# Low-rank stage ahead of the recurrence, gemms in thirds beside it, and an even spread of output projections over the last recurrence

## The chip, the cores and the metric

The kernel runs on one core of a Trainium2 chip. The metric is the device time of one execution in microseconds (us); the time before is the median of three runs. Profiles are of one execution each. Engines: PE is TensorE's matmuls (PEld its weight loads), DVE VectorE, ACT ScalarE, POOL GpSimd, SP SyncE, whose queue issues most DMAs. The granted clock is the share of full TensorE clock that the throttle allowed.

## The reference, cut to what matters

One inference step of a two-layer trunk for a prompt of 1024 tokens and 8 sample streams of 16 tokens, width 1024, all float32. Layer 0 is an RWKV-7 time mixing and an FFN, layer 1 a banded attention and an FFN; every sub-layer is modulated by `silu(c) @ w_ada`. The change lies in the time mixing of layer 0:

```python
r = xr @ w_r;  k = xk @ w_k;  v = xv @ w_v
w_log = -softplus(-(w0 + tanh(xw @ w1) @ w2)) - 0.5      # low rank
a_gate = sigmoid(a0 + (xa @ a1) @ a2)                    # low rank
g = sigmoid(xg @ g1) @ g2                                # low rank
# for each token: the 64x64 state of each of 16 heads
s = s * w_t + (s @ a_t) b_t + v_t k_t ;  y = s @ r_t
y = groupnorm(y) * ln_w + ln_b + bonus
x = x + gate * ((y * g) @ w_o)
```

## The kernel before, in words

The 1152 tokens (1024 of the prompt, 128 of the samples) are cut into three blocks of 384. Precise products are made of float32r halves: a weight tile is loaded raw (512 KB), ACT copies it to a high half (`whi`), DVE subtracts for the low half (`wlo`), and each product is three matmuls (`mm3`, line 257). A gemm of one output tile (`gemm`, line 263) is 8 k steps, 24 matmuls into one bank `acc`.

**Projection of a block** (`proj`, line 495) is a generator whose steps are its yields: the low-rank stage `proj_lora` (line 545; seven yields: three first-stage products, two of gates, two of outputs), then `proj_k` (670), then the inverses of the block's three windows in alternation with `proj_r` (523), then `proj_v` (638); each of the three big ones is 8 gemms, with one yield after each. Results go to DRAM (`spill`, `save`) and are loaded again by the recurrence.

**The recurrence** goes window by window (128 tokens; 9 windows, each in two halves of the heads, so 18 units). A unit is prepared (`win_prep`, line 785: masked products in two banks `G`), run (`win_run`, `win_state`: for each of two chunks of 64 tokens a product X, an eviction, U with the inverse TT, an eviction, D, and the new state, in two banks `st`), summed in bank `Y`, and normed (`win_post`, line 1018: mean and variance by matmuls into two more `st` banks; the result goes to DRAM as `yg`). The two units of a pair are woven, so that one waits while the other works. The inverse of a window (`inverses`, line 773) is a chain of its own: products, a DMA to DRAM, a solve of 15 steps on DVE, DMAs, and four merges in `st` banks.

**The modulation steps** (`ada_steps`, line 195): 8 units of four loads of 512 KB, each with 4 small matmuls, and an end with a copy on ACT. 8 steps are taken in `proj_v` of block 2, 24 are left. They share the raw buffers of `rawtile` (line 227) with the weights; behind block 2 there are two such buffers (line 1170).

**The order** is written in `layer0a` (line 1156). Block 0 is projected alone. For blocks 1 and 2, `alternate` (line 1061) takes 5 steps of the recurrence of the block before, then 4 of the projection. Behind block 2 the last six units run, 5 steps of them to 2 of `early` (line 1173), which holds the 24 modulation steps and then `outproj` (line 1130) of blocks 0 and 1; `outproj` of block 2 comes last. The program is built with `schedule_with_timeline_sim=True`: the instructions are put in order for each engine from this text, and what an engine executes need not be in the text's order.

An output projection loads `yg` (8 tiles `mr`, split into 16 tiles `mx`), runs 8 gemms with the weights `rw_o`, adds the residual, and ends with a square sum whose result is stored as `rr`.

Of the kernel before, what the change touches and what calls it, by code (L numbers as in the profile page):

```python
# [16 lines left out]
NB = 3  # L17
TB = 384
KF = 8
KAPPA = float(np.exp(-0.5))  # L20


# [119 lines left out]
class Trunk:  # L142
# [44 lines left out]
        return self.ps.tile([128, 512], dt, tag=tag, name=self.nm(tag), bufs=bufs)  # L187


    def step(self, n=1):  # L190

        for _ in range(n):
            next(self.ada, None)

    def ada_steps(self, units, tag="aux", bufs=1, tile=None):

        nc = self.nc
        for u in units:
            ps = self.bank(tag, bufs)
            for i in range(4):  # L200
                w = (tile or self.rawtile)()
                nc.sync.dma_start(w[:, :1024], self.a["wada"][u, i])
                c = slice(i // 2 * 256, i // 2 * 256 + 256)
                for q in range(4):
                    mm(nc, ps[32 * q:32 * q + 32, c], self.scT[:, i % 2 * 4 + q, :], w[:, q * 256:q * 256 + 256], i % 2 == 0, i % 2 == 1)
                if i < 3:
                    yield
            sb = (tile or self.rawtile)()[:, :512]
            nc.scalar.activation(sb, ps, AF.Copy)
            for j in range(4):  # L210
                mm(nc, ps[:, j * 16:(j + 1) * 16], sb[:, j * 128:(j + 1) * 128], self.C("qs"), True, True)
            pv = ps[:, 0:64].rearrange("p (j n) -> p j n", n=16)[:, :, 0:9]
            bo = PAR["bada"] + u * 4
            bv = self.par[:, bo:bo + 4].rearrange("p (j o) -> p j o", o=1).broadcast_to([128, 4, 9])
            nc.vector.tensor_tensor(self.mod[:, u * 4:u * 4 + 4, :], pv, bv, ALU.add)
            yield
# [46 lines left out]
    def gemm(self, out, W, hi, lo, m=128):  # L263

        whi, wlo = W
        for k in range(8):
            s = slice(k * m, (k + 1) * m)
            self.mm3(out, whi[:, s], wlo[:, s], hi[k], lo[k], k == 0, k == 7)


    def sq_open(self):
        return Ctx()
# [250 lines left out]
    def proj_r(self, b, hi, lo):  # L523

        nc = self.nc
        for f in range(8):
            W = self.wunit(self.pp, self.a["rw_r"][f])
            pz = self.bank("acc", 2)
            self.gemm(pz[:, :TB], W, hi, lo)
            kp = self.ev("ag", 2)  # L530
            self.load(kp, "kp", b, f)
            ex = self.ev("rr", 2)
            self.load(ex, "cs", b, f)
            nc.scalar.activation(ex, ex, AF.Exp, scale=-KAPPA)
            nc.vector.scalar_tensor_tensor(kp, pz[:, :TB], self.P("rk", f), kp, ALU.mult, ALU.mult)
            nc.vector.tensor_tensor(ex, ex, pz[:, :TB], ALU.mult)
            self.spill("r", b, f, ex)
            aux = self.bank("aux", 1)
            mm(nc, aux[:, :TB], self.C("bo"), kp, True, True)
            bn = self.ev("e0", 3)  # L540
            nc.scalar.activation(bn, aux[:, :TB], AF.Copy)
            self.save("bn", b, f, bn)
            yield
# [94 lines left out]
    def proj_v(self, b, hi, lo):  # L638

        nc = self.nc  # L640
        for f in range(8):
            W = self.wunit(self.pp, self.a["rw_v"][f])
            pz = self.bank("acc", 2)
            self.gemm(pz[:, :TB], W, hi, lo)
            if b in (2,):
                self.step(1)
            vv = self.ev("vv", 2)
            self.load(vv, "bn", b, f)
            v = self.ev("e0", 3)
            nc.scalar.activation(v, pz[:, :TB], AF.Copy)  # L650
            nc.vector.tensor_tensor(vv, vv, pz[:, :TB], ALU.mult)
            nc.scalar.activation(vv, vv, AF.Identity, bias=self.P("lnb", f))
            self.spill("v", b, f, vv)
            pt = self.bank("aux", 1)
            for w in range(3):
                nc.tensor.transpose(pt[:, w * 128:(w + 1) * 128], v[:, w * 128:(w + 1) * 128], self.C("ident"))
            vt = self.ev("e0", 3)
            nc.scalar.activation(vt, pt[:, :TB], AF.Copy)
            for e in range(2):
                nc.sync.dma_start(self.sv[b][:, :, e, f, :].rearrange("w p d -> p w d"),  # L660
                                  vt.rearrange("p (w e d) -> p e w d", w=3, e=2)[:, e])
            yield
# [7 lines left out]
    def proj_k(self, b, hi, lo):  # L670

        nc = self.nc
        self.eend = self.eends[b]
        for f in range(8):
            W = self.wunit(self.pp, self.a["rw_k"][f])
            pz = self.bank("acc", 2)
            self.gemm(pz[:, :TB], W, hi, lo)
            iv = self.ev("rr", 2)
            self.load(iv, "cs", b, f)
            ag = self.ev("ag", 2)  # L680
            self.load(ag, "a", b, f)
            ext = self.pp.tile([128, 408], F32, tag="ext", name=self.nm("ext"), bufs=1)
            for s, sx, n, i in self.spans(b):
                ev = ext[:, sx].rearrange("p (g t) -> p g t", t=n + 1)
                nc.gpsimd.memset(ev[:, :, 0:1], 1.0)
                nc.scalar.activation(ev[:, :, 1:], iv[:, s].rearrange("p (g t) -> p g t", t=n), AF.Exp, scale=-KAPPA)
                nc.gpsimd.tensor_copy(self.eend[:, f, i:i + ev.shape[1]], ev[:, :, n])
            nc.scalar.activation(iv, iv, AF.Exp, scale=KAPPA)
            sq = self.ev("sq", self.nsq)
            kk = self.ev("kk")  # L690
            nc.scalar.activation(sq, pz[:, :TB], AF.Square, scale=self.P("kk", f))
            aux = self.bank("aux", 1)
            mm(nc, aux[:, :TB], self.C("bo"), sq, True, True)
            kp = self.ev("kp")
            nc.scalar.activation(kp, ag, AF.Identity, bias=self.oka[:, f:f + 1], scale=self.P("ka", f))
            inv = self.ev("inv", self.nsq)
            nc.vector.tensor_scalar(inv, aux[:, :TB], 1e-24, None, ALU.max)
            nc.scalar.activation(inv, inv, AF.Ln)
            nc.scalar.activation(inv, inv, AF.Exp, scale=-0.5)
            nc.vector.tensor_tensor(kp, kp, pz[:, :TB], ALU.mult)  # L700
            self.save("kp", b, f, kp)
            nc.vector.scalar_tensor_tensor(kk, pz[:, :TB], self.P("kk", f), inv, ALU.mult, ALU.mult)
            nc.vector.tensor_tensor(ag, ag, kk, ALU.mult)
            for s, sx, n, i in self.spans(b):
                seg = kk[:, s].rearrange("p (g t) -> p g t", t=n)
                nc.vector.scalar_tensor_tensor(seg, seg, -1.0, ext[:, sx].rearrange("p (g t) -> p g t", t=n + 1)[:, :, 0:n],
                                               ALU.mult, ALU.mult)
            self.spill("kk", b, f, kk)
            nc.vector.tensor_tensor(ag, ag, iv, ALU.mult)
            self.spill("b", b, f, ag)  # L710
            nc.vector.tensor_tensor(iv, iv, kp, ALU.mult)
            self.spill("k", b, f, iv)
            yield
# [304 lines left out]
    def win_post(self, w, hf, R):  # L1018
# [11 lines left out]
        mm(nc, cen, self.C("cen"), y, True, True)  # L1030
        nc.scalar.activation(y, cen, AF.Square)
        yield
        var = self.bank("st", 2)
        mm(nc, var, self.C("bo"), y, True, True)
        nc.scalar.activation(y, var, AF.Ln, bias=self.eps[:, 1:2], scale=1.0 / 64)
        nc.scalar.activation(y, y, AF.Exp, scale=-0.5)
# [93 lines left out]
    def outproj(self, b):  # L1130
# [12 lines left out]
        for f in range(8):  # L1143
            W = self.wunit(pp, self.a["rw_o"][f])
            pz = self.bank("acc", 2)
            self.gemm(pz[:, :TB], W, hi, lo)
            x = self.ev("rr")
            nc.sync.dma_start(x, self.a["x"][b][:, f, :])
            o = self.ev("e0")
            self.residual(256 if b == 2 else TB, f, 16, o, x, pz[:, :TB])  # L1150
            nc.sync.dma_start(self.x1[:, f, cols], o)
            self.sq_add(st, o)
            yield
        nc.sync.dma_start(self.rr[:, cols], self.sq_done(st))

    def layer0a(self, ctx):
# [4 lines left out]
        with ExitStack() as c2:  # L1161
# [2 lines left out]
                pass  # L1164
            for b in range(1, NB):
                w = self.windows([(w, hf) for w in range(3 * b - 3, 3 * b) for hf in range(2)])
                for _ in self.alternate(w, self.proj(b), 5, 4):
                    pass
        self.tail_open(ct)
        self.nraw, self.nhi, self.nlo = (2, 2, 2)  # L1170
        self.nmix, self.nmr = 16, 2

        def early():
            for _ in range(32):
                if next(self.ada, StopIteration) is StopIteration:
                    break
                yield
            for b in range(2):
                yield from self.outproj(b)
        for _ in self.alternate(self.windows([divmod(int(x), 2) for x in '12 13 16 14 15 17'.split()]), early(), 5, 2):  # L1180
            pass
        cw.close()
        for _ in self.outproj(2):
# [743 lines left out]
```

## Time and profile before

| what | value |
|---|---|
| median of 3 runs | 3878.44 us (3875.95 to 3879.47) |
| the profiled execution | 3879.81 us; its span 3878.0 us |
| mean granted clock | 0.926 |
| block 0 alone (first weights of block 1's low-rank stage are loaded at 277 us) | 0 to 277 us |
| blocks 1 and 2 with the recurrence of the block before | 277 to 985 us |
| the last recurrence and the output projections | 985 to 1342 us |
| everything else (two FFNs, attention) | 1342 to 3878 us |
| DMA moved | 552.31 MB, mean 142 GB/s |

The profile gives busy time of the engines, the granted clock, and for each idle time of an engine what ended it. A busy PE is not PE at its peak: at half clock the same matmuls keep it busy for twice as long, so busy share and clock are read together.

### The profile page before, as it was taken

The numbers are of one execution on the slowest core, as the hardware profiler recorded it, in microseconds if no ns is written. First come the engines' busy times: TensorE is split into PE (matmuls) and PEld (weight loads), VectorE is DVE, ScalarE is ACT, GpSimd is POOL, SyncE is SP. The second block draws the span as 40 slices with busy tenths as digits, with TensorE's granted clock in tenths as the row PEclk, the third lists the DMA queues.
The fourth block names the chain that finished last, engine by engine and source line by source line (L and its number), as shares of the span: only waits on it lengthen the run. The fifth ranks groups of instructions, "written<-read, shape, count | busy, mean of one in ns | idle before, by whom it ended". The sixth has DMA issues, their size and how long they took to land.

```text
span 3878.0 us, 72281 instructions
## 1 busy us (share of the span) xinstructions
PE 3545.9 (91%) x28614; PEld 3130.7 (81%) x28614; DVE 2292.3 (59%) x4388; ACT 1570.7 (41%) x2966; POOL 570.8 (15%) x473
## 2 busy tenths in 40 slices
PE   6789889988889799999999999889889799999999
PEld 4677777867657689999887879677677799999898
DVE  4667566765435765555456842666675764555567
ACT  5555555544213533333311353465654533333310
POOL 0000000000000255444000100000000264453000
PEclk8896899798679989999999999899999899999999
DMA  5775676676646522222755113444554322222521
GB/s 205 229 237 159 182 220 170 176 219 185 185 142 194 175 71 71 75 77 77 270 192 187 68 59 100 140 141 141 150 191 162 127 79 74 74 75 92 170 84 71
DMA packets 429443, 552.31 MB, mean 142 GB/s; under 512 B 128432, under 2 KB 297520, under 8 KB 424624
## 3 DMA queue, kind: packets, MB, share of 16 engines
q1 hardware_dynamic: 374960, 528.80, 42.8%
q10 hardware_dynamic: 54144, 18.89, 2.1%
q8 instruction: 225, 3.69, 0.4%
q14 instruction: 114, 0.93, 0.1%
HBM read 413.42 MB, written 134.12 MB: 141 GB/s over the span
## 4 chain that ended last, share of the span: by engine, by line
PE 67%; DMA 11%; DVE 7%; ACT 4%; issue 2%; SPq 1%; POOL 0%; ACTq 0%; DVEq 0%; POOLq 0%
PE S L139 31%; PE PT L139 15%; PE acc L139 10%; PE st L139 3%; PE O L139 2%; PE G L139 2%; DVE h L255 1%; PE PT L1753 1%; PE Y L139 1%; PE aux L139 1%; DMA TT<-Z 1%; DMA raw<-in_wada 1%; DMA mr<-yg 1%; DMA yg<-y 1%; DMA rr<-sf_cs 1%
## 5 line engine op out<-in xcount | busy, mean ns | idle before, releaser
L139 PE MATMUL S<-h,w 128*128 128x320 f32 (+1 forms) x4944 | 696.9, 300 | 17.9 <-DVE h L255 8.3
L139 PEld LDWEIGHTS S<-h,w 128*128 128x128 f32 x4944 | 675.5, 192 | 26.0 <-DVE h L255 13.3
L139 PE MATMUL S<-h,wh 128*128 128x320 f32 (+1 forms) x2844 | 529.7, 338 | 12.7 <-DVE h L1123 6.8
L139 PE MATMUL acc<-mx,whi 128*128 128x384 f32 x1728 | 497.4, 366 | 30.3 <-ACT mx L254 12.7
L139 PEld LDWEIGHTS S<-h,wh 128*128 128x128 f32 x2844 | 455.7, 189 | 69.2 <-issue 13.3
L254 ACT ACTIVATE w<-rq 128x512 fp32r<-128x512 f32 x308 | 192.1, 629 | 502.4 <-PE S L139 199.3
L255 DVE TENSOR_TENSOR w<-rq,w 128x512 fp32r<-128x512 f32 x308 | 270.6, 882 | 199.1 <-ACT w L254 198.4
L139 PEld LDWEIGHTS acc<-mx,whi 128*128 128x128 f32 x1728 | 332.6, 201 | 60.5 <-ACT mx L254 15.6
L139 PE MATMUL PT<-h,w 128*128 128x320 f32 (+1 forms) x2448 | 355.0, 300 | 15.1 <-ACT w L254 6.9
L139 PEld LDWEIGHTS PT<-h,w 128*128 128x128 f32 x2448 | 337.4, 192 | 18.9 <-ACT w L254 7.1
L139 PE MATMUL acc<-mx,wlo 128*128 128x384 f32 x864 | 311.3, 361 | 6.6 <-DVE wlo L255 6.5
L139 PE MATMUL PT<-h,wh 128*128 128x320 f32 (+1 forms) x1428 | 287.6, 345 | 9.6 <-DVE wh L255 3.9
L1312 POOL TENSOR_TENSOR t<-t,t 128x576 f32<-128x576 f32 (+1 forms) x132 | 216.1, 1637 | 414.2 <-ACT t L1319 291.7
L139 PEld LDWEIGHTS PT<-h,wh 128*128 128x128 f32 x1428 | 234.2, 191 | 39.0 <-issue 6.9
L255 DVE TENSOR_TENSOR wlo<-raw,whi 128x1024 fp32r<-128x1024 f32 x114 | 139.9, 1230 | 96.4 <-ACT whi L254 89.3
L139 PEld LDWEIGHTS acc<-mx,wlo 128*128 128x128 f32 x864 | 172.5, 200 | 14.0 <-DVE wlo L255 9.6
L254 ACT ACTIVATE whi<-raw 128x1024 fp32r<-128x1024 f32 x114 | 119.5, 1054 | 143.0 <-PE acc L139 96.4
L255 DVE TENSOR_TENSOR h<-h,h 128x1024 fp32r<-128x1024 f32 (+4 forms) x112 | 122.9, 1112 | 84.7 <-ACT h L254 69.7
L254 ACT ACTIVATE h<-h 128x1024 fp32r<-128x1024 f32 (+4 forms) x112 | 103.2, 935 | 164.1 <-DMA h<-sd 105.3
L254 ACT ACTIVATE wh<-rq 128x512 fp32r<-128x512 f32 x124 | 74.8, 626 | 230.6 <-PE S L139 146.3
L1312 DVE TENSOR_TENSOR t<-S,t 128x576 f32<-128x576 f32 (+1 forms) x116 | 86.4, 745 | 128.5 <-PE S L139 128.5
L1379 DVE TENSOR_TENSOR h<-h,S 128x640 f32<-128x640 f32 (+1 forms) x150 | 112.1, 752 | 79.4 <-PE S L139 79.2
(423 smaller groups left out, 5712.9 us busy)
## 6 DMA issues: line engine op xcount, KB each, us to landing
h<-in_wada SPq DMA_DIRECT2D x64, 512.0 KB, 6.3
rq<-in_wg SPq DMA_DIRECT2D x88, 256.0 KB, 2.6
rq<-in_wu SPq DMA_DIRECT2D x88, 256.0 KB, 2.6
rq<-in_wd SPq DMA_DIRECT2D x88, 256.0 KB, 3.0
raw<-in_wada SPq DMA_DIRECT2D x32, 512.0 KB, 4.6
kc<-in_ck SPq DMA_DIRECT2D x16, 1024.0 KB, 5.1
vc<-in_cv SPq DMA_DIRECT2D x16, 1024.0 KB, 7.2
sd<-t SPq DMA_DIRECT2D x88, 160.0 KB, 1.9
```

The costliest lines, as they stand in the source:

```text
L139: return nc.tensor.matmul(out, lhsT, rhs, start=start, stop=stop)
L254: self.nc.scalar.activation(hi, x, AF.Copy)
L255: self.nc.vector.tensor_tensor(lo, x, hi, ALU.subtract)
L1312: eng.tensor_tensor(out, x, y, ALU.add)
L1379: nc.vector.tensor_tensor(y, y, d, ALU.add)
L1753: nc.tensor.transpose(pt[:, j * 128:(j + 1) * 128], P[:, j * 128:(j + 1) * 128], self.C("ident"))
```

## The change

Five edits, one of them used at several places:

- `gemm_steps` replaces `gemm` in `proj_r`, `proj_v`, `proj_k` and `outproj`. It is the same 24 matmuls, with a yield after the third and the sixth k step; a gemm is now three steps.
- For blocks 1 and 2, seven steps of the projection (the low-rank stage) are taken ahead of the alternation, and the alternation is 2 steps of the recurrence to 3 of the projection.
- The variance in `win_post` takes a bank of `G` in place of one of `st`.
- Behind block 2, `early` alternates `outproj(0)` and the modulation steps one to one, then `outproj(1)`; the last recurrence takes 1 step to 2 of `early`.
- From there on the load of a modulation step is written one step ahead (`fetch_ahead`).

```diff
+LOW = 7
...
+        def load(u, i):
+            w = (tile or self.rawtile)()
+            nc.sync.dma_start(w[:, :1024], self.a["wada"][u, i])
+            return w
+        todo = [(u, i) for u in units for i in range(4)]
+        ahead = None
...
-                w = (tile or self.rawtile)()
-                nc.sync.dma_start(w[:, :1024], self.a["wada"][u, i])
+                w = ahead or load(*todo.pop(0))
+                ahead = load(*todo.pop(0)) if todo and self.fetch_ahead else None
...
+    def gemm_steps(self, out, W, hi, lo):
+
+        whi, wlo = W
+        for k in range(8):
+            s = slice(k * 128, (k + 1) * 128)
+            self.mm3(out, whi[:, s], wlo[:, s], hi[k], lo[k], k == 0, k == 7)
+            if k in (2, 5):
+                yield
...
-            self.gemm(pz[:, :TB], W, hi, lo)
+            yield from self.gemm_steps(pz[:, :TB], W, hi, lo)
...
-        var = self.bank("st", 2)
+        var = self.bank("G", 2)
...
-                for _ in self.alternate(w, self.proj(b), 5, 4):
+                p = self.proj(b)
+                for _ in range(LOW):
+                    next(p)
+                for _ in self.alternate(w, p, 2, 3):
                     pass
         self.tail_open(ct)
+        self.fetch_ahead = True
...
         def early():
-            for _ in range(32):
-                if next(self.ada, StopIteration) is StopIteration:
-                    break
-                yield
-            for b in range(2):
-                yield from self.outproj(b)
-        for _ in self.alternate(self.windows([divmod(int(x), 2) for x in '12 13 16 14 15 17'.split()]), early(), 5, 2):
+            yield from self.alternate(self.outproj(0), self.ada, 1, 1)
+            yield from self.outproj(1)
+        for _ in self.alternate(self.windows([divmod(int(x), 2) for x in '12 13 16 14 15 17'.split()]), early(), 1, 2):
             pass
```

More of the change, by code (lines that the diff above doesn't have):

```diff
@@ L187, in bank @@
         return self.ps.tile([128, 512], dt, tag=tag, name=self.nm(tag), bufs=bufs)
+    fetch_ahead = False
     def step(self, n=1):
@@ L643, in proj_v @@
             pz = self.bank("acc", 2)
-            self.gemm(pz[:, :TB], W, hi, lo)
+            yield from self.gemm_steps(pz[:, :TB], W, hi, lo)
             if b in (2,):
@@ L676, in proj_k @@
             pz = self.bank("acc", 2)
-            self.gemm(pz[:, :TB], W, hi, lo)
+            yield from self.gemm_steps(pz[:, :TB], W, hi, lo)
             iv = self.ev("rr", 2)
@@ L1145, in outproj @@
             pz = self.bank("acc", 2)
-            self.gemm(pz[:, :TB], W, hi, lo)
+            yield from self.gemm_steps(pz[:, :TB], W, hi, lo)
             x = self.ev("rr")
```

## The prediction

> **What bounds the kernel now.** I read the page first: span, engine shares, and the slices with the granted clock.
>
> ```profile
> span 3878.0 us, 72281 instructions
> PE 3545.9 (91%) x28614; PEld 3130.7 (81%) x28614; DVE 2292.3 (59%) x4388; ACT 1570.7 (41%) x2966; POOL 570.8 (15%) x473
> PE   6789889988889799999999999889889799999999
> PEclk8896899798679989999999999899999899999999
> ```
>
> TensorE bounds the kernel: 91% busy, the next engine 59%. A slice is 97 us, so the change touches only slices 1 to 14, up to 1345 us; what follows (the first FFN, the attention, the second FFN) is left as it is and I forecast nothing for it. In the early slices both rows are lower than later. The stages there, in one table of the stretches (columns: stretch, length, then busy us and count of PE, PEld, DVE, ACT, sometimes POOL, then granted clock, DMA share, GB/s):
>
> ```profile
> 84.00:115.00 31.00, 21.80 (x65) 14.53 (x63) 23.79 (x36) 21.87 (x40) 0.00 (x0) 0.70 0.66 218
> 332.00:400.00 68.00, 61.38 (x564) 49.95 (x563) 47.89 (x111) 28.37 (x54) 0.00 (x0) 0.53 0.49 142
> 684.00:735.00 51.00, 48.40 (x473) 38.37 (x472) 40.94 (x83) 28.17 (x53) 0.00 (x0) 0.56 0.59 173
> 400.00:621.00 221.00, 199.77 (x2367) 167.47 (x2366) 146.46 (x325) 122.28 (x237) 2.90 (x19) 0.92 0.68 200
> 735.00:985.00 250.00, 221.82 (x2705) 182.74 (x2702) 149.44 (x332) 119.12 (x236) 6.15 (x30) 0.92 0.71 201
> 985.00:1176.00 191.00, 162.55 (x1784) 118.55 (x1784) 72.28 (x191) 43.18 (x88) 0.00 (x0) 0.68 0.56 156
> 1236.00:1345.00 109.00, 84.47 (x409) 75.50 (x408) 76.75 (x135) 54.33 (x101) 19.69 (x16) 0.91 0.58 185
> ```
>
> The first three rows are the second half of the low-rank stage (gates and outputs, `proj_lora`) of blocks 0, 1 and 2; the next two are the gemms of blocks 1 and 2 beside the recurrence of the block before; then comes the last recurrence with the modulation steps, and last what is left of the output projections. Three things stand out. The same low-rank half takes 31 us alone, 68 and 51 us beside the recurrence's preparation, and there the clock is 0.53 and 0.56. The last recurrence runs for 191 us at 0.68 with no gemm beside it. After it, 109 us hold little but output projections.
>
> The text's order is a priority and not the order of execution: the zeroing matmul of the first recurrence unit, which stands in the text behind the whole of block 0, runs at 2.40 us.
>
> ```profile
> 2.40 0.79 PE L139 MATMUL Y<-zr 128*128 128x512 f32 x1 [2.40 <-ACT zr L735]
> ```
>
> So an edit that only moves steps in the text moves the time only where readiness and buffers let it. I price each part from what stands in its way.
>
> **A. The low-rank stage ahead (LOW = 7).** Seven steps are exactly `proj_lora`: three first-stage products, two gates, two outputs. What lies between them in blocks 1 and 2 is the preparation of the next recurrence units (tile G) and merges of the last inverse (tile st). First three rows of PE alone for the tile acc, then two for G, then two of all engines for st:
>
> ```profile
> 84.00:115.00 31.00, 21.80 (x65) 0.70 0.66 218
> 332.00:400.00 68.00, 27.17 (x68) 0.53 0.49 142
> 684.00:735.00 51.00, 25.10 (x66) 0.56 0.59 173
> 332.00:400.00 68.00, 27.08 (x128) 0.53 0.49 142
> 684.00:735.00 51.00, 18.98 (x96) 0.56 0.59 173
> 332.00:400.00 68.00, 9.66 (x368) 8.62 (x368) 2.80 (x8) 2.75 (x9) 0.53 0.49 142
> 684.00:735.00 51.00, 6.01 (x311) 5.33 (x312) 1.14 (x4) 2.38 (x8) 0.56 0.59 173
> ```
>
> The acc matmuls are the same 64 or so each time. If the stage runs alone it takes block 0's 31 us: (68 - 31) + (51 - 31) = 57 us less. The displaced work, 27.1 + 19.0 + 9.7 + 6.0 = 62 us of PE at a clock of about 0.545, then stands beside the gemms at 0.92: 62 x 0.545 / 0.92 = 37 us. Net 57 - 37 = 20 us. The other end is 0: the preparation is ready, and may slip into the idle places of the low-rank stage as before. I take 14, nearer to block 0's row, since that is the same stage with nothing beside it. Its DMAs (the loads of the low-rank weights, the saves of its results) now go ahead of the preparation's loads on SP's queue; I cost that at nothing, because the first state step runs only here, behind the merges:
>
> ```profile
> 415.43 1.15 PE L139 MATMUL st<-UV,XL 128*64 128x64 f32 x32
> 747.29 1.15 PE L139 MATMUL st<-UV,XL 128*64 128x64 f32 x32
> ```
>
> That is 15 and 12 us after the low-rank stage ends. If this cover goes, a late start is paid at most with those stretches' idle time, below.
>
> The Trainium skill, page "TensorE: Matmul & The Clock Gate", section "Why this matters for your kernels", says that a TensorE kept busy some 4 us without a break gets the full clock. This trace differs: 48.4 of 51 us busy, and 0.56 granted. By the rule moving the preparation would win no clock, and this part would come to 62 - 57 = 5 us lost.
>
> **B. Gemms in thirds, 2:3 instead of 5:4, and the variance in bank G.** No matmul is added. Each gemm (24 matmuls) gets two more places for a recurrence step, and the inverses alternate with thirds of `proj_r`, in block 0 too, where I cost it at nothing (the gemms of `proj_v` follow without a wait on it). What can be won is the idle time of the two gemm stretches, 221 - 199.8 + 250 - 221.8 = 49 us. Of it these waits are what a finer weave or a freed st bank would shorten (in 400 to 985: total, times, longest):
>
> ```profile
> PE st L139 <- ACT y L1028: 5.1, 2, 4.8
> PE st L139 <- ACT UV L943: 4.2, 4, 2.2
> PE st L139 <- ACT y L1031: 3.7, 3, 1.4
> PE st L139 <- ACT xs L934: 2.8, 3, 1.4
> PE G L139 <- DVE XL L819: 5.8, 1, 5.8
> ```
>
> The first four sum to 16 us. The last is the price of the bank: the variance matmul now waits in PE's queue until a mask multiply on DVE has freed a G bank, once 5.8 us, and queued behind it is every later matmul. I take half of the 16, 8 us; the ends are 16 won and the loss of rival 3.
>
> **C. The end of the stage.** Now the 24 remaining modulation steps come first, then output projections 0 and 1, then 2 after the last window. Rows of the tile raw, and of SP's queue (start, us):
>
> ```profile
> L202 SPq DMA_DIRECT2D raw<-in_wada x24: 327/338/859, 1016.6 to 1165.8; - x24
> L209 ACT ACTIVATE raw<-aux x6: 592/597/606, 1039.3 to 1171.7; 128x512 f32<-128x512 f32 x6
> 1171.74 6.47 SPq L247 DMA_DIRECT2D raw<-in_rw_o  x3
> 1246.17 0.34 SPq L1154 DMA_DIRECT2D rr<-rms  x1
> 1267.49 0.33 SPq L247 DMA_DIRECT2D raw<-in_rw_o  x1
> 1275.89 0.33 SPq L247 DMA_DIRECT2D raw<-in_rw_o  x1
> 1287.03 0.33 SPq L1154 DMA_DIRECT2D rr<-rms  x1
> 1341.78 0.32 SPq L1154 DMA_DIRECT2D rr<-rms  x1
> 1244.77 0.37 ACTq L1043 DMA_DIRECT2D yg<-y  x1
> ```
>
> Everything goes through two raw buffers: 24 loads and 6 copies in 1171.7 - 1016.6 = 155 us, 5.17 us a buffer; the weights of a projection running alone, with one more load between the two quoted, (1275.89 - 1267.49) / 2 = 4.2 us. A projection ends where its rr is stored: 0 at 1246, 1 at 1287 (41 us later), 2 at 1342 (55 us later). The windows end at 1245.
>
> Alternating 1:1 puts projection 0 among the modulation steps. The buffers still carry 30 + 8 = 38 tiles: 30 x 5.17 + 8 x 4.2 = 189 us, to 1206; with an estimated 6 us for the last tile's split and gemm (one and a half of the 4.2) projection 0 ends at 1212, projection 1 at 1253 beside the last windows, projection 2 at 1308: 34 us earlier. PE has room: projection 0's 8 gemms are 41 us at most by projection 1's row, and 985 to 1176 has 28 us idle and runs at 0.68. The modulation load a step ahead is no new buffer, so it can only pull the pace towards 4.2; behind it in SP's queue stand the recurrence's loads. What the queues pay now (SP, PE, PE):
>
> ```profile
> SPq L202 <- PE aux L139: 42.6, 13, 10.2
> PE aux L139 <- DMA raw<-in_wada: 17.8, 10, 4.2
> PE G L139 <- DMA BK<-sp_k: 6.6, 3, 5.0
> ```
>
> Its bounds: at 4.2 for all 38, projection 0 ends at 1182, and then the windows decide (rival 2); the loss is rival 4.
>
> **Sum.** 14 + 8 + 34 = 56 us. The profiled execution took 3879.8 us (1.8 outside the span): 3823.8. It lies 1.4 above the median, so 3822.
>
> **Rivals.**
> 1. Nothing moves: the order follows readiness, the buffers carry the same 38 tiles, and projection 0 stays behind. For it: the matmul at 2.40 us. Against: 109 us of projections behind the windows. 3878.
> 2. More is won. With gemms among its steps the last recurrence runs at 0.92 instead of 0.68: 162.6 x (1 - 0.68 / 0.92) = 42 us, the windows end at 1203, projection 1 at 1182 + 41 = 1223, projection 2 at 1278, 64 us earlier. With A at 20 and B at 16: 100 us, 3778. Against: the chain's evictions and DMAs don't follow the clock.
> 3. The thirds cost clock. A gemm that is broken twice and then waits for a recurrence step leaves PE idle in the middle. The stretches hold 199.8 + 221.8 = 422 us of PE at 0.92. At 0.80, half way to the 0.68 of the recurrence without gemms, that is 422 x (0.92 / 0.80 - 1) = 63 us; with A and C, 63 - 48 = 15 slower: 3893. It decides below a clock of 0.83. For it stands the skill's same page, section "HAM oscillation — how this bites in real kernels": run all K tiles through before PE waits. Against: two acc banks hold a second gemm ready.
> 4. Slower through the raw buffers. A matmul whose load is late holds PE's queue and with it the recurrence: 17.8 / 10 = 1.78 us a time, now in 10 of 24 steps. If all 38 tiles pay it, the pace is 5.17 + 1.78 = 6.95: 264 us, projection 0 ends at 1287, projection 2 at 1383, 41 us late; with A and B, 41 - 22 = 19 slower: 3897. C turns to a loss above (1341.8 - 55 - 41 - 6 - 1016.6) / 38 = 5.87 us a tile, the whole above 6.45.
>
> **How the numbers follow.** Forecast 0.50, rival 1 0.12, rival 2 0.21, rival 3 0.06, rival 4 0.11. A difference of 0.2% (8 us) is about what a measurement of this kernel can tell from none. Faster 0.71, same 0.12, slower 0.17. The range is 3770 (a little past rival 2) to 3890 (past rival 1, and the milder part of rivals 3 and 4).
>
> **What would show it.** A: gates and outputs of blocks 1 and 2 in about 31 us, no G among them. B: a clock of 0.92 or more and less than 49 us idle in the gemm stretches. C: weights of the output projections loaded between 1016 and 1206 on the scale of now, the gap from the last yg to the last rr well under today's 97 us. I am wrong if the pace of the raw buffers passes 5.87 us, if the windows end later after the end of block 2's gemms than now, or if the gemm stretches lose clock.

## The result, and the profile after

The changed kernel takes 3939.84 us (median of 4 runs, 3935.16 to 3945.3) against 3877.19 us for the kernel before on the same chip: a ratio of 1.0172, 95% interval 1.0152 to 1.0192, so 63 us slower where 56 us faster was forecast, and outside the forecast range of 3770 to 3890 us. First the page of the changed kernel: span, engines, and the slices with the granted clock.

```profile
span 3933.3 us, 72242 instructions
PE 3573.6 (91%) x28614; PEld 3148.4 (80%) x28614; DVE 2296.6 (58%) x4388; ACT 1579.2 (40%) x2972; POOL 576.4 (15%) x473
PE   5889989898799689999999999888889889999999
PEclk8887988798779679999999999999999999999999
```

The same 28,614 matmuls, the same busy share and much the same clock, in a span 55.3 us longer. A slice is now 98 us. The 6 in the clock's row that stood in the 11th slice, at the last recurrence without gemms, stands in the 14th, behind 1278 us. The stages, cut where they fall in this kernel (columns as in the prediction):

```profile
332.00:387.00 55.00, 50.06 (x532) 39.41 (x532) 44.53 (x102) 27.74 (x54) 0.00 (x0) 0.61 0.60 168
649.00:726.00 77.00, 65.43 (x763) 49.54 (x761) 47.26 (x107) 45.51 (x77) 0.00 (x0) 0.65 0.51 157
735.00:985.00 250.00, 218.08 (x2494) 183.19 (x2492) 136.13 (x291) 112.57 (x225) 4.98 (x28) 0.91 0.65 186
1190.00:1330.00 140.00, 117.58 (x1144) 89.59 (x1143) 68.13 (x152) 36.21 (x63) 0.00 (x0) 0.82 0.41 129
1330.00:1395.00 65.00, 42.68 (x179) 38.17 (x180) 48.56 (x90) 31.84 (x64) 19.54 (x16) 0.74 0.43 141
```

The gates and outputs of blocks 1 and 2 now take 55 and 77 us (before 68 and 51), not 31. In 735 to 985 us TensorE is about as busy as before at about the same clock, but it executes 2494 matmuls where it executed 2705. The gemms' are as many (548 in tile acc, before 552); fewer are those of the recurrence and the inverses (1240 in st for 1319, 294 in G for 336). In 400 to 621 us the gemms have more than before (537 for 504) and st has fewer (872 for 1076). So the projections come early and the recurrence late. The last weights of block 2's `proj_v` are loaded at 937.13 us (before 976.19), the last recurrence store `yg` and the ends `rr` of the three output projections stand here (start in us):

```profile
937.13 0.58 SPq L257 DMA_DIRECT2D raw<-in_rw_v  x1
1325.97 0.37 ACTq L1062 DMA_DIRECT2D yg<-y  x1
1205.76 0.33 SPq L1173 DMA_DIRECT2D rr<-rms  x1
1268.70 0.33 SPq L1173 DMA_DIRECT2D rr<-rms  x1
1393.44 0.32 SPq L1173 DMA_DIRECT2D rr<-rms  x1
```

Projections 0 and 1 end 40 and 18 us earlier than before (1246, 1287). The recurrence ends 81 us later (1326 against 1245), and projection 2, which needs it, 52 us later: nearly the whole loss of the span. The question for the experiments is what holds the recurrence. I call the last store of block 0's, of block 1's and of the last recurrence the three marks: before 653, 977, 1245; changed 715, 1088, 1326.

### The profile page after: what moved, and what is told of

Read it like the earlier page. It is cut to its first block, busy times and chain, and to the rows that moved or that the text cites. A ratio compares the mean times of both kernels' runs of the same rounds, so it can differ in the third digit from the quotient of the medians.

```text
span 3933.3 us, 72242 instructions
## 1 busy us (share of the span) xinstructions
PE 3573.6 (91%) x28614; PEld 3148.4 (80%) x28614; DVE 2296.6 (58%) x4388; ACT 1579.2 (40%) x2972; POOL 576.4 (15%) x473
## 4 chain that ended last, share of the span: by engine, by line
PE 68%; DMA 10%; DVE 7%; ACT 5%; issue 2%; SPq 1%; POOL 1%; ACTq 0%; DVEq 0%; POOLq 0%
PE S L140 31%; PE PT L140 15%; PE acc L140 11%; PE st L140 3%; PE G L140 2%; PE O L140 2%; DVE h L265 1%; PE PT L1772 1%; PE Y L140 1%; PE aux L140 1%; DMA TT<-Z 1%; DMA Z<-T 1%; DMA yg<-y 1%; ACT pts L1773 0%; DMA L<-ld 0%
## 5 line engine op out<-in xcount | busy, mean ns | idle before, releaser
L140 PE MATMUL acc<-mx,whi 128*128 128x384 f32 x1728 | 515.1, 378 | 66.4 <-ACT mx L264 28.7
L140 PEld LDWEIGHTS acc<-mx,whi 128*128 128x128 f32 x1728 | 345.6, 209 | 102.9 <-ACT mx L264 34.4
```

The source lines that it names most:

```text
L140: return nc.tensor.matmul(out, lhsT, rhs, start=start, stop=stop)
```

## The experiments

Each was timed in turn with the kernel before on the same chip; the ratio is to that, with its 95% interval. Line numbers differ by up to 19 between kernels, since the edits add lines.

**1. Inverses thinner in the text?** In the changed kernel an inverse alternates with thirds of `proj_r`, one to one. If its merges were crowded, one step to three thirds would mend it.

```diff
-        yield from self.alternate(self.inverses(b), self.proj_r(b, *r))
+        yield from self.alternate(self.inverses(b), self.proj_r(b, *r), 1, 3)
```

> The changed kernel with one edit: the inverses alternate 1 step to 3 thirds of proj_r, as many as they had to a whole gemm before. Theory (ring): the merges of the inverses, now written three times as close, stand ahead of recurrence steps in the two-bank ring st and hold both banks while they wait for their solve and its DMAs. It expects the last yg of block 0's recurrence near 655 us instead of 714, that of block 1's near 985 instead of 1088, and a time of 3800 to 3860. Rival (priority): the recurrence is late because the low-rank stage and the gemm thirds stand ahead of it; it expects no move, 3920 to 3950. Rival (tail): the raw buffers in the last recurrence cost it; 3920 to 3950.

3933.55 us, 1.0124 (1.0092 to 1.0156); marks 774, 1097, 1324. The inverses did move (that of block 2's last window began its solve at 1047 us instead of 1074), but the recurrence did not come earlier with them: block 0's last store came 59 us later, the other two marks moved by 9 us at most. That theory fell.

**2. The merges of the inverses out of `st`.** The four merges take banks of `G`, and the variance goes back to `st`.

```diff
-        m = self.bank("st", 2)
+        m = self.bank("G", 2)
...
-        var = self.bank("G", 2)
+        var = self.bank("st", 2)
```

> The changed kernel with the four banks of a merge taken from G instead of st, and the variance back in st. The order of the steps in the text is that of the changed kernel. Theory (ring): X, U and D no longer stand behind a merge, only the preparations do, a pair ahead of need: block 1's last yg near 1000 us, 3820 to 3880. Rivals (priority, tail): 3920 to 3960.

3937.18 us, 1.0131 (1.0100 to 1.0162); marks 718, 1067, 1341. No better. What I had not thought of is that this puts another chain into `G` (see 11 to 13).

**3 and 4. The tail alone, and the blocks alone.** The change cut in two: the kernel before with `early`, the 1:2, the thirds in `outproj` and the load ahead; and the changed kernel with the old tail.

> The kernel before with the change's tail alone: outproj in thirds, outproj(0) one to one with the modulation steps, 1 to 2, loads a step ahead; variance in st, blocks 0 to 2 as before. Theory (ring) and the rival (priority): the tail is sound where the recurrence comes to it in time, 3835 to 3865, last yg of all near 1240 us. Rival (tail): 3900 to 3940.

> The change without its tail: behind block 2 all is as before (whole gemms in outproj, 24 modulation steps first, 5 to 2). Theory (ring) and the rival (priority): block 1's last yg stays near 1088 us, the old tail follows it, 3930 to 3990. Rival (tail): the gain of the two blocks shows, 3840 to 3870.

The tail alone: 3884.81 us, 1.0008 (0.9990 to 1.0027), no difference; marks 646, 978, 1276, projections at 1190, 1241, 1342. The blocks alone: 3920.31 us, 1.0083 (1.0051 to 1.0116); marks 724, 1090, 1320. Neither time lies in a range that was expected. Both halves fail to give what was forecast, so there is more than one cause.

**5 to 8. Which of the blocks' edits.** The changed kernel with only the variance put back in `st`; then the kernel before with one edit each: the variance in `G`; the seven low-rank steps ahead (5:4 and whole gemms kept); thirds and 2:3.

```diff
# 5: changed kernel                     # 6: kernel before, the same line reversed
-        var = self.bank("G", 2)
+        var = self.bank("st", 2)
# 7: kernel before
+                p = self.proj(b)
+                for _ in range(7):
+                    next(p)
-                for _ in self.alternate(w, self.proj(b), 5, 4):
+                for _ in self.alternate(w, p, 5, 4):
# 8: kernel before, gemm_steps in proj_k, proj_r, proj_v
-                for _ in self.alternate(w, self.proj(b), 5, 4):
+                for _ in self.alternate(w, self.proj(b), 2, 3):
```

> The changed kernel with one thing undone: the variance of the output norm goes back from a G bank to the st banks. Three theories of why blocks 1 and 2 now end their recurrence late. Variance bank: the centred copy holds one of the two st banks while the variance waits for a G bank behind the chunk preparations and the inverse products, so one st bank is left for the state products and the merges; then this kernel gets most of it back, about 3880 to 3895, with block 1's last store of the recurrence near 1000 (before 977, changed 1088). Priority by the low-rank steps ahead: stays at 3925 to 3940. Thinner spread by thirds and 2:3: stays at 3925 to 3940.

> The kernel before with one thing of the change: the variance of the output norm takes a G bank in place of an st bank. Variance bank: slower by 25 to 40 us, block 0's last store of the recurrence at 700 or later (before 653). Priority by the low-rank steps ahead, and thinner spread by thirds: no difference within 10 us.

> The kernel before with one thing of the change: the seven low-rank steps of the next block stand ahead of the alternation of recurrence and projections; whole gemms and 5:4 as before, the variance in st. Priority by the low-rank steps ahead: slower by 20 to 40 us, with the recurrence of block 0 ending past 680. Variance bank and thinner spread: the same, or faster by up to the 14 us that the prediction gave this part.

> The kernel before with one thing of the change: the projections' gemms in thirds and 2:3 in place of whole gemms and 5:4; no low-rank steps ahead, the variance in st, the tail as before. Thinner spread: slower by 20 to 40 us, with the inverses' or the recurrence's ends of block 0 later by tens of us. Variance bank and priority by the low-rank steps: the same within 10 us.

| kernel | median us | ratio (interval) | marks |
|---|---|---|---|
| 5 changed, variance in `st` | 3887.12 | 1.0015 (1.0002 to 1.0028) | 696, 1046, 1281 |
| 6 before, variance in `G` | 3910.11 | 1.0074 (1.0059 to 1.0089) | 640, 1012, 1302 |
| 7 before, low-rank ahead | 3853.88 | 0.9920 (0.9897 to 0.9942) | 651, 990, 1265 |
| 8 before, thirds and 2:3 | 3876.13 | 0.9983 (0.9965 to 1.0001) | 667, 1006, 1250 |

The variance's bank is the blocks' cost: put back it recovers 1.57 of the 1.72%, alone it costs 0.74%. The low-rank steps ahead are a gain, the thirds make no difference to speak of; both rival theories fell. But the variance theory missed its own mark: block 0's recurrence in kernel 6 ends at 640 us, earlier than before, where I expected 700 or later. Number 5's block 1 ends at 1046 us, where I expected about 1000. The bank costs, and not by the way I thought.

**9 and 10. The two good edits together, and low-rank ahead with the tail.** Kernel 9 is the kernel before with low-rank ahead, thirds and 2:3; kernel 10 is number 7 with the change's tail.

> The kernel before with the low-rank steps ahead, thirds and 2:3 in the blocks; the variance in st, the tail as before. If the parts add (low-rank alone -25.7, thirds alone -3.4): 3845 to 3860, block 1's last store of the recurrence by 1006. If low-rank steps ahead and thirds hinder each other: 3870 to 3890 and that store at about 1046, as in the changed kernel with the variance put back.

> The kernel before with two things of the change: the seven low-rank steps ahead and the tail; whole gemms and 5:4 in the blocks, the variance in st. If the parts add (low-rank alone -25.7 and tail alone +5.2 against the kernel before): 3855 to 3865, the last windows ending about 31 us later than with the low-rank steps alone (1265), at 1290 or more. If the tail gives its gain back only where the windows begin early: the time falls below 3850.

Kernel 9: 3858.36 us, 0.9938 (0.9910 to 0.9966); marks 691, 1030, 1224, projection 2 at 1327. The time adds up within the intervals, though block 1's last store comes at 1030 us and not by 1006; and with kernel 7 it beats both kernels of this case. A late mark in blocks 0 and 1 is thus no loss in itself: 691 and 1030 are later than before (653, 977). Kernel 10: 3876.67 us, 0.9979 (0.9959 to 0.9999); marks 656, 999, 1282: with low-rank ahead the tail costs about 0.6%, more than it did alone. Neither expectation had that.

**11. What the variance's bank costs by.** If the centred copy holding an `st` bank were to blame, taking both banks of the norm from `G` would free `st` and mend it.

```diff
-        cen = self.bank("st", 2)
+        cen = self.bank("G", 2)
...
-        var = self.bank("st", 2)
+        var = self.bank("G", 2)
```

> The kernel before with both banks of the output norm, the centred copy's and the variance's, taken from G, so that the norm holds no st bank. If the variance in G costs because the centred copy holds an st bank while the variance waits: the 30 us are gone, 3875 to 3892, block 1's last store of the recurrence by 990. If a wait for a G bank costs by itself (the norm's matmuls in front of others on the engine, or the chunk preparations kept from their banks): 3905 or more.

3991.65 us, 1.0292 (1.0261 to 1.0322); marks 702, 1083, 1389. Four times the cost: the held `st` bank is not the cause, the use of `G` is. (The norm's two `st` banks are not two others, as "into two more `st` banks" above may read, but turns of the one pair that the state chain and the merges use.) In the kernel before, two things share the two `G` banks: the preparation of the units, and the products that open a window's inverse (`Aab<-G`, copied out by ACT). The latter run ahead of the recurrence. Here are ACT's copies for the middle window of block 1 and the norms of the last units of block 0 (start, us), first in the kernel before:

```profile
598.70 0.60 ACT L768 ACTIVATE Aab<-G 128x512 f32<-128x512 f32 x1
600.22 0.60 ACT L768 ACTIVATE Aab<-G 128x512 f32<-128x512 f32 x1
603.81 3.00 ACTq L845 DMA_DIRECT2D L<-ld  x4
617.18 0.70 ACT L1035 ACTIVATE y<-st,eps 128x512 f32<-128x512 f32 x1
637.78 0.69 ACT L1035 ACTIVATE y<-st,eps 128x512 f32<-128x512 f32 x1 [3.71 <-DMA TT<-Z]
```

Then with the variance in `G` (kernel 6):

```profile
615.87 0.69 ACT L1035 ACTIVATE y<-G,eps 128x512 f32<-128x512 f32 x1 [0.78 <-PE G L139]
634.75 0.69 ACT L1035 ACTIVATE y<-G,eps 128x512 f32<-128x512 f32 x1 [3.59 <-PE G L139]
636.00 0.58 ACT L768 ACTIVATE Aab<-G 128x512 f32<-128x512 f32 x1
642.65 0.60 ACT L768 ACTIVATE Aab<-G 128x512 f32<-128x512 f32 x1 [0.92 <-PE G L139]
650.98 2.29 ACTq L845 DMA_DIRECT2D L<-ld  x4
```

And with both of the norm's banks in `G`:

```profile
693.25 0.60 ACT L1031 ACTIVATE y<-G 128x512 f32<-128x512 f32 x1 [0.65 <-PE G L139]
695.26 0.69 ACT L1035 ACTIVATE y<-G,eps 128x512 f32<-128x512 f32 x1 [0.81 <-PE G L139]
697.74 0.60 ACT L768 ACTIVATE Aab<-G 128x512 f32<-128x512 f32 x1
705.71 0.60 ACT L768 ACTIVATE Aab<-G 128x512 f32<-128x512 f32 x1 [0.55 <-PE G L139]
```

Before, the inverse's products are out at 600 us, 38 us ahead of the last norm. With the variance in `G` they come right behind that norm, at 636 us, and with both banks there again right behind it, at 698. The reading: the two banks of a name go round in the order of the text, so whatever asks for `G` behind the norm waits until the norm, at the end of the recurrence, has had its turn. The text bears this out: number 6 asks for the two `G` banks of these opening products directly behind the variances of both units of block 0's last window, while in the kernel before they follow the preparation of that window, and no norm stands in the round. The load that starts the solve (`L<-ld`) goes from 603.81 to 650.98, and block 1's first store from 793 to 854 us. Little of this shows as TensorE standing idle for a bank of `G`: in 400 to 985 us of kernel 6 TensorE's weight loads waited for the variance's evacuation for 2.5 us in all.

```profile
PEld G L139 <- ACT y L1035: 2.5, 2, 1.6
```

**12 and 13. That reading tested.** Kernel 13 is number 6 with the opening products of the inverse in the gemms' `acc` banks, out of the round; kernel 12 is its control, the kernel before with that move alone.

```diff
# win_first (12, and 13 on top of number 6)
-        G = self.bank("G", 2)
+        G = self.bank("acc", 2)
```

> The control for the next run: the kernel before, with the products that open an inverse taken from the gemms' two acc banks in place of G. Whatever the cause of the variance's price: within 15 us of before, since G was free for them (evicted at 599 and 600 us for the middle window of block 1).

> The kernel before with the variance in G and the products that open an inverse out of G, in acc. If the variance costs because the two G banks go round in the text's order, so that these products stand behind the norm of the last unit of the block before (evicted at 636 and 643 us, right behind that norm at 635): they are evicted by 610 again, and 15 us or more of the 30 come back, 3880 to 3895 or as near to the control. If the norm costs by its own wait, or through the chunk preparations alone: 3905 or more.

Control: 3955.28 us, 1.0196 (1.0167 to 1.0225); kernel 13: 3942.14 us, 1.0150 (1.0120 to 1.0181). The control missed widely, since `acc` turned out to be no free place either: the low-rank stage of block 1 begins at 335 us instead of 277. But beside it the variance in `G` costs nothing any more: 0.5% below the control, with intervals that overlap a little, where it cost 0.74% with the products in `G`. Kernel 13's products are out at 614 and 623 us, ahead of the norms at 630 and 647. So the reading holds as far as these two kernels can be compared; by its time alone (3942, "3905 or more") number 13 would fit its rival too, and only the control tells them apart. The control shows the same thing in another pair of banks. In its text the opening products of block 0's last window stand in `acc` ahead of `proj_v`; between 262 and 304 us TensorE executes no gemm matmul, and the first one, at 306.73, comes 1 us behind the copy that frees one of these banks (305.71). What I can't give from these runs is the price in absolute time with the products in a place that costs nothing.

**14 to 17. Why the tail gives its gain back.** The kernel before with the tail's order alone (no load ahead); with the load ahead alone; with the tail at one to one in place of one to two; and the changed kernel with the variance in `st` and one to one.

```diff
# 14: the changed tail
-        self.fetch_ahead = True
# 15: the tail as before
+        self.fetch_ahead = True
# 16 and 17
-        for _ in self.alternate(self.windows([...]), early(), 1, 2):
+        for _ in self.alternate(self.windows([...]), early(), 1, 1):
```

> The kernel before with the tail's order alone: output projections 0 and 1 in thirds and the modulation steps spread evenly through the last windows at 1:2, no load a step ahead. If the spread itself makes the windows late: their end at about 1276 (before 1245), the time within 10 us of before. If the second raw buffer's loads do it: the windows end at 1245 to 1255 and the time falls by 20 to 34 us.

> The kernel before with the modulation loads a step ahead in the tail and nothing else. If the spread makes the windows late: they end at 1245 or up to 15 us earlier here, the time 0 to 15 us below before. If the loads ahead do it: they end at 1260 or later and the time is 0 to 20 us above before.

> The kernel before with the change's tail at one window step to one step of projections and modulation, in place of one to two. With one to two the projections were over at 1241 us and the windows ran on alone until 1276. If the gain was given back because the projections run out before the windows do: here they last to the windows' end, which comes by 1260, and the time falls 8 to 20 us below before. If every third beside the windows costs them what it takes off behind them: the windows end earlier than 1276, the projections as much later, and the time stays within 6 us of before.

> The changed kernel with two things other: the variance back in st, and the tail at one to one. If the projections ran out too early in the tail: below 3858, which the blocks' edits give with the old tail. If the thirds beside the windows only move time: 3858 to 3887, between that and the changed kernel with the variance back.

| kernel | median us | ratio (interval) | last mark | projections 0, 1, 2 |
|---|---|---|---|---|
| before (its profile) | 3878.44 | 1 | 1245 | 1246, 1287, 1342 |
| 3 tail alone | 3884.81 | 1.0008 (0.9990 to 1.0027) | 1276 | 1190, 1241, 1342 |
| 14 order alone | 3900.98 | 1.0044 (1.0028 to 1.0060) | 1295 | 1202, 1250, 1362 |
| 15 loads ahead alone | 3885.97 | 1.0000 (0.9985 to 1.0016) | 1257 | 1233, 1285, 1341 |
| 16 tail, one to one | 3883.25 | 0.9994 (0.9973 to 1.0016) | 1263 | 1230, 1290, 1347 |
| 17 changed, `st`, one to one | 3874.15 | 0.9983 (0.9965 to 1.0001) | 1262 | 1223, 1278, 1336 |

The order is what makes the windows late (number 14), the load ahead takes some of that back. Number 14's windows end later (1295 us) and its time is longer by 16 us, more than either expectation had; number 15's windows end at 1257, between its two. Spreading the projections thinner (16) lets the windows end 13 us sooner and projection 1 end 49 us later, for the same time: the theory that only the early end of the projections was at fault fell, time is moved. With the blocks' gain (17) one to one is better than one to two (number 5) by some 0.3%, and still no better than the old tail (number 9).

Where the time goes in the tail is seen in the table of stretches: first the kernel before, then the tail alone, which has one stretch more.

```profile
1060.00:1120.00 60.00, 51.16 (x485) 34.98 (x486) 19.31 (x49) 9.85 (x19) 0.00 (x0) 0.60 0.52 144
1120.00:1180.00 60.00, 49.50 (x651) 32.53 (x649) 21.50 (x59) 12.61 (x23) 0.00 (x0) 0.80 0.48 149
1245.00:1280.00 35.00, 33.03 (x173) 30.37 (x172) 21.61 (x32) 13.66 (x20) 0.00 (x0) 0.97 0.83 260
```

```profile
1060.00:1120.00 60.00, 52.80 (x587) 38.85 (x582) 23.32 (x47) 15.85 (x27) 0.00 (x0) 0.91 0.70 207
1120.00:1180.00 60.00, 58.29 (x560) 41.72 (x561) 31.50 (x79) 14.28 (x27) 0.00 (x0) 0.86 0.64 187
1245.00:1280.00 35.00, 19.50 (x176) 11.16 (x174) 8.36 (x21) 4.42 (x7) 0.00 (x0) 0.57 0.17 50
1280.00:1345.00 65.00, 44.41 (x185) 39.95 (x186) 47.82 (x90) 32.13 (x65) 19.53 (x16) 0.71 0.42 140
```

Between 1060 and 1180 TensorE was idle for 19.3 us and is now for 8.9: 10.4 us filled, at a better clock. Between 1245 and 1280 it was idle for 2.0 us and is now for 15.5: 13.5 us opened, at a clock of 0.57, because the projections are used up and the last windows run alone. In between, each unit of the recurrence goes slower beside thirds than beside modulation steps. The first and the fourth store of the last recurrence, before and then in the tail alone:

```profile
1067.64 0.38 ACTq L1043 DMA_DIRECT2D yg<-y  x1
1182.68 0.43 ACTq L1043 DMA_DIRECT2D yg<-y  x1
```

```profile
1073.19 0.42 ACTq L1061 DMA_DIRECT2D yg<-y  x1
1217.85 0.37 ACTq L1061 DMA_DIRECT2D yg<-y  x1
```

That is (1182.68 - 1067.64) / 3 = 38 us a unit before and (1217.85 - 1073.19) / 3 = 48 with the thirds. The books of the stage: the windows take 298 us instead of 268 from block 1's last store, what stands behind them 66 instead of 97: +30 and -31.

## Why the prediction was wrong, point by point

**B, the variance's bank: the step that failed.** I priced the bank as "the variance matmul now waits in PE's queue until a mask multiply on DVE has freed a G bank, once 5.8 us". Alone it cost 0.74%, 30 us against the 3880 of its runs; on top of low-rank and thirds 1.45% (number 4 against 9), some 56 us, and 1.57% (the changed kernel against 5). I looked for what the norm would wait for. The price lies on the other side: who waits behind the norm for the two banks. TensorE's wait rows hardly show it (2.5 us in number 6); it shows in the order, the inverse's products behind the norm. In the changed kernel the text puts the middle window's opening products ahead of those norms, and the preparation of block 1's first unit directly behind the last of them. There the same is seen at that preparation: its first masked product (line 838) runs right behind the last norm of block 0, while in number 9, with the variance in `st`, it runs 56 us earlier and ahead of the norm. First the changed kernel, then number 9:

```profile
702.86 0.69 ACT L1054 ACTIVATE y<-G,eps 128x512 f32<-128x512 f32 x1
704.04 0.43 DVE L838 TENSOR_TENSOR XL<-G,cst 64x256 f32<-64x256 f32 x1
```

```profile
647.96 0.43 DVE L838 TENSOR_TENSOR XL<-G,cst 64x256 f32<-64x256 f32 x1
677.25 0.69 ACT L1054 ACTIVATE y<-st,eps 128x512 f32<-128x512 f32 x1
```

No run took the preparation out of the round, so for the changed kernel this way is seen, and not tested by itself.

The Trainium skill, page "Perfetto Trace Analysis", section "Optimizing Tensor Performance", says under "Matmuls" that independent matmul groups should rotate through different banks, so that the evacuation of one overlaps the next. No run here tests that overlap: the weight loads' wait for the variance's evacuation is the 2.5 us above, and the 30 us of number 6 come with the order in which one pair serves two independent chains.

**B, the thirds.** Forecast -8 with the variance, measured -0.17% (-0.35 to +0.01%) without it, some 7 us: that fits, but can hardly be told from nothing. The inverses, costed "at nothing", are not where the loss is: put thinner they changed the time by about half a per cent (number 1). The two gemm stretches of number 8 are these:

```profile
400.00:621.00 221.00, 200.17 (x2304) 168.05 (x2302) 146.37 (x331) 119.13 (x232) 3.03 (x18) 0.92 0.71 205
735.00:985.00 250.00, 224.80 (x2615) 185.98 (x2614) 144.42 (x324) 117.53 (x234) 8.54 (x30) 0.93 0.68 195
```

They kept their clock, so rival 3 did not come. Their idle time went from 49 to 46 us, so little of the 16 us of waits named there was won.

**A, right in sign, wrong in mechanism.** Number 7 gave -0.80% (-1.03 to -0.58%), 22 to 40 us, more than the 14 forecast and than its end of 20. But the gates and outputs do not run alone. The same halves in number 7, all engines, and then TensorE's work for the tile G in them:

```profile
331.00:388.00 57.00, 52.97 (x453) 42.58 (x453) 44.41 (x102) 25.70 (x46) 0.00 (x0) 0.53 0.59 166
672.00:717.00 45.00, 39.59 (x211) 32.28 (x210) 37.85 (x87) 25.55 (x46) 0.00 (x0) 0.58 0.64 183
331.00:388.00 57.00, 22.20 (x120) 0.53 0.59 166
672.00:717.00 45.00, 14.91 (x97) 0.58 0.64 183
```

57 and 45 us, with 22.2 and 14.9 us of the preparation still inside: 17 us gained by these two stretches, not 57. The clock stayed at 0.53 and 0.58. The Trainium skill's rule of some 4 busy microseconds for the full clock (page "TensorE: Matmul & The Clock Gate", section "Why this matters for your kernels") again differs from the trace: 53.0 of 57 us busy, and 0.53 granted; within it, from 352 to 368 us, 15.8 of 16 us busy without a gap between matmuls, and 0.50 granted. The profile of number 7 is of its slowest run, 3875.14 us, only 5 us below the profiled run before, with its last `rw_v` load at 948.81 us (27 earlier than before); where the timed gain of 26 us lies it can't show, and this stays open.

**C, the term of -34 was nil.** The projections' times were sized well: 1212 and 1253 forecast for 0 and 1, 1190 and 1241 measured in number 3. So the raw buffers held, and rival 4 fell. What failed is the step "projection 1 at 1253 beside the last windows, projection 2 at 1308", which leaves the windows' end at 1245 and puts 55 us behind it. The windows ended at 1276, and projection 2 took 66 us from there, at 0.71. "PE has room" compared 41 us of gemms with 28 us idle and a low clock; but the recurrence is a chain on the same engine, and beside thirds a unit of it takes 48 us instead of 38 (that each of its products waits behind a third in TensorE's queue is the likely way, argued and not shown one by one). Rival 2 had the sign of the clock right (0.60 to 0.91) and the windows' end wrong.

**The sum.** From number 9 (-0.62%) the variance's bank adds 1.45 and the tail 0.89: +1.72%. As parts alone the three were +0.74, +0.08 and about -0.97: -0.15%. So bank and tail both cost more together with the earlier projections than alone. That more work is ready beside the recurrence, which can then only lose its place, fits the marks, but was not tested by itself. My own list of what would make me wrong had the sign to look for ("if the windows end later after the end of block 2's gemms than now": 1326 - 937 = 389 us against 1245 - 976 = 269); I gave it no price.

## What to carry to other kernels

Before a tile is moved to another pair of banks, list all that goes round in that pair and ask which of them runs ahead: from then on it can't run ahead of the slowest one, and TensorE's wait rows may hardly name it. Idle time beside a dependent chain is not room for other work on the same engine: price what each product of the chain then waits, and ask what is left to cover the chain's end. Of this change the low-rank steps ahead (0.992), with or without the thirds (0.994), were worth keeping; the other two edits were not.

## What the runs showed of the hardware

The granted clock did not follow the busy share of a stretch: 0.53 with TensorE busy for 53.0 of 57 us, 0.91 with 52.8 of 60. In number 7 it was 0.50 from 352 to 368 us, with TensorE busy for 15.8 of these 16 us. The 2.9% of number 11 is the price of an order and not of added work: both banks of each unit's norm came from another pair, with not one matmul added.
